# A hybrid encoder layer on one core: how 256-column products read their moving operand, and how a norm writes its parts

## The chip, the cores and the metric

The kernel runs on one core of a Trainium2 chip. The metric is the device time of one execution in microseconds (us), without anything that the host does before it: weights are arranged on the host, outside the time. Five engines work side by side, each with its own queue in program order: the TensorE (PE) for matmuls, with its weight loads (PEld); the VectorE (DVE); the ScalarE (ACT); the GpSimd (POOL); and the SyncE (SP), which here issues DMAs. Matmuls read a stationary operand (the weights that are loaded first) and a moving operand (whose columns stream through) from SBUF and write to PSUM, which ACT and DVE read.

## The reference

One encoder layer on a sequence of 512 positions and width 1024, in float32:

```
h  = RMSNorm(x);  q,k,v,g,u,sv,a_ret,a_sgu = split(h @ w_in)      # 512,512,1024,1024,1024,1024,1024,1024 columns
y_ret = (LayerNorm(retention(rotary(q), rotary(k), v)) * silu(g)) @ w_ret_o   # 4 heads, key 128, value 256, both directions
y_sgu = (gelu(u) * (w_spatial · LayerNorm(gelu(sv)) + b)) @ w_sgu_o           # chunks of 128 positions, 4 groups
x1 = x  + RMSNorm((sig(a_ret) * y_ret + sig(a_sgu) * y_sgu) @ w_out)
c  = conv3(RMSNorm(x1) @ w_up) + conv_b;  a,b = split(c)                     # 2 x 2816 columns, 3 taps along the sequence
y  = x1 + RMSNorm((gelu(a) * b) @ w_down)
```

## The kernel before, in words

**Products in three parts.** TensorE takes float32 here in a rounded form (`float32r`). To keep the accuracy, every operand is split into a high and a low part: `split` (lines 95 and 111) rounds a copy on ACT to get the high part and subtracts it on DVE to get the low one. Each product is then three matmuls into the same PSUM bank: high x high, high x low, low x high (`mm3`, lines 240 to 242, and the same written out elsewhere). A weight block streams in by DMA (`raw<-wall`, issued by SP), is split by ACT and DVE, and is used; `w_get` looks a few blocks ahead.

**512 and 256 columns.** Most products have a moving operand of 512 columns. Others have 256, for two reasons: a head's value width is 256, and large products are done by a scheme of seven products of half size in the place of eight (`Pair`, line 773, and `products`, line 1187), with sums and differences of operand blocks made by DVE and GpSimd (`x_forms`, `h2_forms`, `w_form`, `w_down`, `down_forms`). In a `Pair` a weight form is stationary and a 256-column block of x, or of the forms S1 to S4, moves. In the down projection the activations are stationary and 256 columns of w_down move; `add_whole` (line 1203) does the blocks left over.

**Reading in turn.** A moving operand of 512 columns is read as two halves in turn: column 0, column 256, column 1, column 257, and so on, so the product comes out with its columns in that mixed order. Where the order matters later, either the reader of PSUM takes every second column (`in_turn`) and writes the two halves in their places (`two`), or the weights were mixed on the host so that the product comes out in natural order (`_turns`). The 256-column products of the second norm's output (`h2h`, `h2l`) in `Pair.x` and in `early` also read in turn, as 128 columns out of each half of a 512-column tile. All other 256-column products read 256 neighbouring columns: the heads' `scores`, `states` and `values` (240 matmuls), `Pair` on x and its forms (1008) and on the forms S1 to S4 of the up projection (384), line 1187 (756) and line 1203 (192).

**Order of the work.** The q and k products come first, then per head v, scores, states and values among the other input products; then u (from 209 us), the two gated branches (to 430 us), the output product with the second norm (430 to 480 us), the up projection (to 690 us) and the down projection. In the second norm, `norms` (line 949 and on) makes mean squares on ACT, a reciprocal root on GpSimd and the scaled rows on DVE; `turn` transposes them on PE (line 1009) and writes for each k the high part on ACT (line 1011) and the low part on DVE (line 1014); `h2_rows` (line 1028) writes a float32 copy on ACT, from which `h2_forms` makes S1 to S4. While this goes on, PE does `early`, the first products of the up projection, each of which waits for its k's parts. The scheduler keeps each engine's program order as the code gives it, apart from a few places where the code pins it (`issue_after`).

Tiles are allocated with start offsets of 64 or 192 bytes in some pools (`hi192`, `lo64`, `AT_64`, `AT_192`), which set them apart from each other within 256 bytes.

Of the kernel before, what the change touches and what calls it, by code (L numbers as in the profile page):

```python
# [15 lines left out]
P = 128  # L16
# [31 lines left out]
def tile_block(ctx: ExitStack, tc, xT, x, wall, par, cs, wsp, bsp, gpost, gffn, out):  # L48
# [48 lines left out]
    def two(t):  # L97
        return t.rearrange("p (n c) -> p n c", n=2)

    def turns(t, f=slice(0, 256)):  # L100
        return t.rearrange("p (n c) -> p c n", n=2)[:, f, :]

    def in_turn(o):
        return o.rearrange("p (c n) -> p n c", n=2)
# [398 lines left out]
    def rotary(m):  # L503
# [4 lines left out]
        v.tensor_add(a, a, b)  # L508
        return a

    def parts(src, n, held=True):
        h_, l_ = (hi192(n), lo64(n)) if held else (blk(F32R, n), blk(F32R, n))
        split(h_, l_, src)
        return h_, l_

    hd = {}

    def prep(h):

        k = rotary(4 + h)  # L520
        kp = parts(k, "k")
        q = rotary(h)
        qp = parts(q, "q", False)
        xi = powers(tmp("xi"), xp, xn, h)
        v.tensor_mul(q, q, xi)
        hd[h] = [qp, kp, parts(q, "qx"), k]
# [54 lines left out]
    def scores(h):  # L581
        (qh, ql), (kh, kl) = hd[h][:2]
        dec = powers(tmp("dec"), dp, dn, h)
        sm = []
        for c in range(2):
            s = ps()
            n = slice(c * 256, (c + 1) * 256)
            for i in range(2):
                m = slice((2 * c + i) * P, (2 * c + i + 1) * P)
                mm3(s[:, i * 256 : (i + 1) * 256], kh[:, m], kl[:, m], qh[:, n], ql[:, n], True, True)  # L590
            m = tmp("sm")
            v.scalar_tensor_tensor(
                out=m, in0=s, scalar=DK ** -0.5, in1=dec, op0=ALU.mult, op1=ALU.mult
            )
            sm.append(parts(m, "sm"))
        return sm

    def states(h):
        nh, e = h // 2, slice((h % 2) * DV, (h % 2 + 1) * DV)
        kh, kl = hd[h][3]  # L600
        s = ps()
        for d in range(2):
            for i in range(2):
                t = 2 * d + i
                c = slice(t * P, (t + 1) * P)
                mm3(s[:, d * DV : (d + 1) * DV], kh[:, c], kl[:, c], vh[t, nh][:, e], vl[t, nh][:, e],
                    i == 0, i == 1)
        return parts(s, "st", False)

    def values(h, sm, st):  # L610
        nh, e = h // 2, slice((h % 2) * DV, (h % 2 + 1) * DV)
        xh_, xl_ = hd[h][2]
        for n2 in range(2):
            o = ps()
            for nn in range(2):
                n = 2 * n2 + nn
                oo = o[:, nn * DV : (nn + 1) * DV]
                for i in range(2):
                    c = slice(i * 256 + nn * P, i * 256 + (nn + 1) * P)
                    t = 2 * n2 + i  # L620
                    mm3(oo, sm[n2][0][:, c], sm[n2][1][:, c], vh[t, nh][:, e], vl[t, nh][:, e],
                        i == 0, False)
                c = slice(n * P, (n + 1) * P)
                d = slice((1 - n2) * DV, (2 - n2) * DV)
                mm3(oo, xh_[:, c], xl_[:, c], st[0][:, d], st[1][:, d], False, True)
            for nn in range(2):
                n = 2 * n2 + nn
                oo = o[:, nn * DV : (nn + 1) * DV]
                if (n, nh) not in o_sb:
                    o_sb[n, nh] = blk(n="o")  # L630
                bs = small("bs", 6, 4)
                v.bn_stats(out=bs, in_=oo)
                v.bn_aggr(out=mv[:, n, h, :], in_=bs)
                copy(o_sb[n, nh][:, e], oo)
        rsqrt(orstd[:, h, :], mv[:, :, h, 1], 1.0, NT)
        for n in range(NT):
            ot = o_sb[n, nh][:, e]
            v.tensor_scalar(
                out=ot, in0=ot, scalar1=mv[:, n, h, 0:1], scalar2=orstd[:, h, n : n + 1],
                op0=ALU.subtract, op1=ALU.mult,  # L640
            )
# [115 lines left out]
    class Pair:  # L757
# [3 lines left out]
        def __init__(self, func, alloc, a=None, scale=None):  # L761
            self.func, self.t, self.scale = func, [alloc(), alloc()], scale
            self.h, self.l, self.forms = a or (xh, xl, forms)
            self.b = [ps() for _ in range(3)]

        def product(self, b, act, first, w=None):
            wh, wl = w or w_get()
            o = self.b[b][:, T0]
            for k in range(4):
                c = slice(k * P, (k + 1) * P)  # L770
                h_, l_ = act(k)
                for n, (w_, a_) in enumerate(((wh, h_), (wh, l_), (wl, h_))):
                    self.last = nc.tensor.matmul(  # L773
                        o, w_[:, c], a_, start=first and k == n == 0, stop=k == 3 and n == 2,
                        skip_group_check=True,
                    )
            return o

        def x(self, first, t):
            if self.h is xh:  # L780
                return lambda k: (self.h[first + k][:, t], self.l[first + k][:, t])
            f = slice(t.start // 2, t.stop // 2)
            return lambda k: (turns(self.h[first + k], f), turns(self.l[first + k], f))

        def s(self, n):
            return lambda k: self.forms[n][k]

        def part1(self, apart=False):

            c0, c1 = self.t  # L790

            def second():
                o = self.product(1, self.x(4, T0), True)
                v.tensor_add(c0[:, T0], o, c0[:, T0])

            o = self.product(0, self.x(0, T0), True)
            copy(c0[:, T0], o)
            if not apart:
                second()
            self.product(2, self.s("S1"), True)  # L800
            o = self.product(0, self.s("S2"), False)
            copy(c1[:, T0], o)
            if apart:
                second()
            if self.scale is not None:
                v.tensor_mul(c0[:, T0], c0[:, T0], self.scale[:, T0])

        def part2(self):
            c0, c1 = self.t
            o = self.product(0, self.s("S3"), False)  # L810
            copy(c1[:, T1], o)
            v.tensor_sub(c1[:, T1], self.b[2][:, T0], c1[:, T1])
            self.w = w_get(), w_get()

        def part3(self):
            c0, c1 = self.t
            o = self.product(0, self.x(4, T1), False, self.w[0])
            if self.scale is None:
                copy(c0[:, T1], o)
            else:  # L820
                v.tensor_mul(c0[:, T1], o, self.scale[:, T1])
                nc.scalar.activation(out=c0, in_=c0, func=self.func)
            o = self.product(2, self.s("S4"), False, self.w[1])
            v.tensor_sub(c1[:, T0], o, c1[:, T0])
            if self.scale is not None:
                v.tensor_mul(c1, c1, self.scale)
                nc.scalar.activation(out=c1, in_=c1, func=self.func)
# [168 lines left out]

    h2 = []

    def both(t):
        return t.rearrange("p (c n) -> p c n", n=2)  # L1000

    def turn(t, zs):
        c = slice(t * 64, (t + 1) * 64)
        pf = []
        for n in range(2):
# [3 lines left out]
                nc.tensor.transpose(pf[-1], zs[n][:, f * P : (f + 1) * P], ident)  # L1009
            for k in range(4 * n, 4 * n + 4):  # L1010
                last = nc.scalar.activation(  # L1011
                    out=turns(h2h[k], c), in_=both(pf[k]), func=AF.Copy, scale=col(FFNG + k)
                )
                v.scalar_tensor_tensor(  # L1014
                    out=turns(h2l[k], c), in0=both(pf[k]), scalar=col(FFNG + k), in1=as32(turns(h2h[k], c)),
                    op0=ALU.mult, op1=ALU.subtract,
                )
        if t != 2:
# [3 lines left out]
    def h2_rows(t, pf):  # L1022

        for k in range(KD):
            if t == 0 and k % 2 == 0:
                h2.append(halves("h2"))
            at = (k % 2) * 256 + (t % 2) * P
            nc.scalar.activation(
                out=h2[k // 2][t // 2][:, at : at + P], in_=pf[k], func=AF.Copy, scale=col(FFNG + k)
            )  # L1030

    early_w, early_o = [], []
# [140 lines left out]
    def products(m, j, steps={}, look=LOOK, ahead=None):  # L1173

        for n, (unit, at, act) in enumerate(UNITS):
# [7 lines left out]
            for t in range(2):  # L1183
                c = slice(t * P, (t + 1) * P)
                o = m[n][:, t * 256 : (t + 1) * 256]
                for i, (a_, w_) in enumerate(((ah, wh), (ah, wl), (al, wh))):
                    nc.tensor.matmul(  # L1187
                        o, a_[:, c], w_[:, f], start=j == t == i == 0,
                        stop=j == DP - 1 and i == 2 and n not in (M2, M3, M4), skip_group_check=True,
                    )  # L1190
            steps.get(n, lambda: None)()
# [1 line left out]
    def add_whole(m, t, gs, ws, last=False):  # L1193

        c = slice(t * P, (t + 1) * P)
        for n, b in enumerate(((M2, M3), (M4, M8))[t // 2]):
            o = m[b][:, (t % 2) * 256 : (t % 2 + 1) * 256]
            for g, (wh, wl) in zip(gs, ws):
                for k in range(2):
                    f = slice(k * S + n * 256, k * S + (n + 1) * 256)  # L1200
                    ah, al = whole[2 * g + k]
                    for i, (a_, w_) in enumerate(((ah, wh), (ah, wl), (al, wh))):
                        nc.tensor.matmul(  # L1203
                            o, a_[:, c], w_[:, f], start=b == M8 and t == 2 and g == k == i == 0,
                            stop=last and g == gs[-1] and k == 1 and i == 2, skip_group_check=True,
                        )

# [162 lines left out]
    return a.reshape(a.shape[0] // P, P, a.shape[1])  # L1370


def _turns(a):

    return a.reshape(*a.shape[:-1], 256, 2).swapaxes(-1, -2)


def _pairs(a):
# [108 lines left out]
```

## Time and profile before

| | before |
|---|---|
| time, median of 3 runs | 806.9 us (806.28, 806.9, 809.85) |
| the profiled execution | 809.66 us, span 807.9 us |
| PE busy | 791.6 us, 98% of the span |
| PE weight loads | 735.3 us, 91% |
| DVE busy | 664.9 us, 82% |
| ACT busy | 443.3 us, 55% |
| GpSimd busy | 84.8 us, 11% |
| DMA | 93.24 MB, mean 115 GB/s |

A row of a group reads: line, engine, operation, what is written and from what, the shape, how many, busy time in us, mean duration in ns, idle time before it and what ended it. A row of the timeline reads: start in us, duration in us, engine, line, operation, tiles, shape, how many in a row, and in brackets the idle time before it and who ended that. A row of the chain that ended last gives start, length, engine, tile, line and count. Matmuls overlap, so the listed duration of one is longer than the distance to the next.

### The profile page before, as it was taken

To read this page: it belongs to the slowest core of one execution; us is meant where nothing else is said; L and a number is where in the kernel's file an instruction comes from. 1 tells how busy PE (TensorE), PEld (TensorE's weight loads), DVE (VectorE), ACT (ScalarE), POOL (GpSimd) and SP (SyncE) were. 2 spreads that over 40 slices of the span, in tenths; PEclk is the share of its full clock that TensorE was granted. 3 is DMA by queue.
4 is the path that set the end of the run, shared out by engine and by line. 5 is a ranking of instruction groups with operands and counts; after the bars stand their busy time and mean duration, and the time that the engine had idled before them with its cause. 6 is when DMAs were issued, how large, how long until landed. Compare 5 with 4: busy or idle time off the path is not lost. (4 is left out here: it accounts for less than half of the span.)

```text
span 807.9 us, 13298 instructions
## 1 busy us (share of the span) xinstructions
PE 791.6 (98%) x5163; PEld 735.3 (91%) x5163; DVE 664.9 (82%) x1115; ACT 443.3 (55%) x777; POOL 84.8 (11%) x93
## 2 busy tenths in 40 slices
PE   9989999999999999999999999999999999999996
PEld 7878998998999999999998898899998898999996
DVE  6579897877898787777765669999999989987887
ACT  6455446546676444444444687556656666544442
POOL 0010000010001111132211210110110100000001
PEclk9999999999999999999999999999999999999999
DMA  7743222222233333223359111323333341233244
GB/s 271 249 149 105 72 85 59 79 87 77 105 105 105 105 105 104 80 105 105 124 164 335 54 47 61 105 105 105 105 105 105 105 157 53 79 131 105 97 165 157
DMA packets 29903, 93.24 MB, mean 115 GB/s; under 512 B 3536, under 2 KB 4688, under 8 KB 29840
## 3 DMA queue, kind: packets, MB, share of 16 engines
q1 hardware_dynamic: 27616, 86.76, 31.4%
q0 software_dynamic: 1360, 4.46, 1.6%
q10 hardware_dynamic: 864, 1.18, 0.4%
q8 instruction: 40, 0.66, 0.3%
q14 instruction: 23, 0.19, 0.1%
HBM read 88.19 MB, written 4.19 MB: 114 GB/s over the span
## 5 line engine op out<-in xcount | busy, mean ns | idle before, releaser
L95 ACT ACTIVATE wf<-raw 128x512 fp32r<-128x512 f32 x140 | 85.4, 625 | 97.9 <-PE ps L241 30.6
L111 DVE TENSOR_TENSOR wl<-raw,wh 128x1024 fp32r<-128x1024 f32 (+1 forms) x92 | 109.6, 1200 | 34.0 <-PE ps L773 19.1
L111 DVE TENSOR_TENSOR wf<-raw,wf 128x512 fp32r<-128x512 f32 x140 | 108.7, 788 | 19.9 <-ACT wf L95 18.9
L773 PE MATMUL ps<-sh,wf 128*128 128x256 f32 x640 | 120.9, 278 | 2.0 <-ACT c L95 2.0
L95 ACT ACTIVATE wh<-raw 128x1024 fp32r<-128x1024 f32 (+2 forms) x96 | 93.0, 980 | 31.0 <-DMA raw<-wall 16.0
L773 PEld LDWEIGHTS ps<-sh,wf 128*128 128x128 f32 x640 | 101.7, 188 | 3.1 <-ACT c L95 2.4
L241 PE MATMUL ps<-h2l,wh 128*128 128x512 f32 (+1 forms) x256 | 90.4, 355 | 1.8 <-DVE h2l L1014 1.8
L240 PE MATMUL ps<-h2h,wh 128*128 128x512 f32 (+1 forms) x256 | 90.3, 355 | 0.1
L242 PE MATMUL ps<-h2h,wl 128*128 128x512 f32 (+1 forms) x256 | 90.1, 353 | 0.0
L773 PE MATMUL ps<-sl,wf 128*128 128x256 f32 x320 | 89.0, 278 | 0.0
L554 PE MATMUL ps<-wh,xh 128*128 128x512 f32 x192 | 73.5, 383 | 0.0
L556 PE MATMUL ps<-wh,xl 128*128 128x512 f32 x192 | 73.5, 383 | 0.0
L555 PE MATMUL ps<-wl,xh 128*128 128x512 f32 x192 | 73.4, 382 | 0.0
L773 PEld LDWEIGHTS ps<-sl,wf 128*128 128x128 f32 x320 | 60.1, 188 | 0.4
L1187 PE MATMUL ps<-dl,fh 128*128 128x256 f32 x216 | 59.8, 277 | 0.0
L1187 PE MATMUL ps<-dh,fh 128*128 128x256 f32 x216 | 59.7, 277 | 0.0
L1187 PE MATMUL ps<-dh,fl 128*128 128x256 f32 x216 | 59.7, 277 | 0.0
L241 PEld LDWEIGHTS ps<-h2l,wh 128*128 128x128 f32 x256 | 48.5, 189 | 6.8 <-DVE h2l L1014 2.2
L773 PE MATMUL ps<-xh,wf 128*128 128x256 f32 x288 | 54.5, 279 | 0.0
L95 ACT ACTIVATE dh<-raw 128x768 fp32r<-128x768 f32 (+1 forms) x36 | 33.6, 948 | 37.1 <-DVE raw L213 17.7
L242 PEld LDWEIGHTS ps<-h2h,wl 128*128 128x128 f32 x256 | 48.5, 190 | 5.2
L240 PEld LDWEIGHTS ps<-h2h,wh 128*128 128x128 f32 x256 | 48.3, 189 | 5.2 <-ACT h2h L1011 0.4
(314 smaller groups left out, 2037.1 us busy)
## 6 DMA issues: line engine op xcount, KB each, us to landing
raw<-wall SPq DMA_DIRECT2D x144, 512.0 KB, 3.6
x<-x SPq DMA_DIRECT2D x24, 256.0 KB, 6.0
x<-x POOLq DMA_DIRECT2D x8, 256.0 KB, 2.4
xT<-xT SPq DMA_DIRECT2D x7, 256.0 KB, 5.8
xT<-xT POOLq DMA_DIRECT2D x4, 256.0 KB, 3.4
out<-zg SPq DMA_DIRECT2D x4, 256.0 KB, 2.0
raw<-wall SPq DMA_DIRECT2D x3, 256.0 KB, 4.2
out<-zs ACTq DMA_DIRECT2D x3, 256.0 KB, 2.3
```

The lines of the kernel that those rows point to most:

```text
L95: return nc.scalar.activation(out=o, in_=i, func=AF.Copy)
L111: nc.vector.tensor_sub(lo, src, as32(hi))
L240: nc.tensor.matmul(o, ah, bh, start=start, stop=False, skip_group_check=skip)
L241: nc.tensor.matmul(o, ah, bl, start=False, stop=False, skip_group_check=skip)
L242: nc.tensor.matmul(o, al, bh, start=False, stop=stop, skip_group_check=skip)
L554: nc.tensor.matmul(acc[t], xh[k][:, c], turns(wh[:, f]), start=k == 0, stop=False)
L555: nc.tensor.matmul(acc[t], xh[k][:, c], turns(wl[:, f]), start=False, stop=False)
L556: part_end[0] = nc.tensor.matmul(acc[t], xl[k][:, c], turns(wh[:, f]), start=False, stop=k == KD - 1)
L773: self.last = nc.tensor.matmul(o, w_[:, c], a_, start=first and k == n == 0, stop=k == 3 and n == 2, skip_group_check=True,)
L1187: nc.tensor.matmul(o, a_[:, c], w_[:, f], start=j == t == i == 0, stop=j == DP - 1 and i == 2 and n not in (M2, M3, M4), skip_group_check= ...
```

## The change

Products of 256 columns now read the moving operand as two halves in turn too: in a block of 256, column 0, column 128, column 1, column 129, and so on. Where the result has to be in natural order, what reads it from PSUM takes every second column: the evictions of `Pair` on x (`self.two`), the heads' outputs (line 634 of the kernel before, `copy(o_sb...)`), and the split of the states (`parts_in_turn`). q is split with its two halves of 256 mixed each, so that the scores come out in natural order. w_down's columns are mixed on the host, in blocks of 256. For the second norm, the parts (`h2h`, `h2l`) are written as two runs of 64 columns per transposed block, with every second column read from PSUM, where before the two halves were written alternately and PSUM was read in order; the result in SBUF is the same. The float32 copy `h2` is now mixed likewise and also written in runs of 64.

```diff
-    def turns(t, f=slice(0, 256)):
-        return t.rearrange("p (n c) -> p c n", n=2)[:, f, :]
+    def turns(t, f=None):
+        v_ = t.rearrange("p (n c) -> p c n", n=2)
+        return v_ if f is None else v_[:, f, :]
...
+    def four(t):
+        return t.rearrange("p (i n c) -> p i n c", i=2, n=2)
+
+    def four_in_turn(o):
+        return o.rearrange("p (i c n) -> p i n c", i=2, n=2)
...
+    def parts_in_turn(src, n):
+        h_, l_ = blk(F32R, n), blk(F32R, n)
+        split(four(h_), four(l_), four_in_turn(src))
+        return h_, l_
...
-        qp = parts(q, "q", False)
+        qp = parts_in_turn(q, "q")
...
-                mm3(s[:, i * 256 : (i + 1) * 256], kh[:, m], kl[:, m], qh[:, n], ql[:, n], True, True)
+                mm3(s[:, i * 256 : (i + 1) * 256], kh[:, m], kl[:, m], turns(qh[:, n]), turns(ql[:, n]), True, True)
...
-                mm3(s[:, d * DV : (d + 1) * DV], kh[:, c], kl[:, c], vh[t, nh][:, e], vl[t, nh][:, e],
+                mm3(s[:, d * DV : (d + 1) * DV], kh[:, c], kl[:, c], turns(vh[t, nh][:, e]), turns(vl[t, nh][:, e]),
                     i == 0, i == 1)
-        return parts(s, "st", False)
+        return parts_in_turn(s, "st")
...
-                mm3(oo, xh_[:, c], xl_[:, c], st[0][:, d], st[1][:, d], False, True)
+                mm3(oo, xh_[:, c], xl_[:, c], turns(st[0][:, d]), turns(st[1][:, d]), False, True)
...
-                copy(o_sb[n, nh][:, e], oo)
+                copy(two(o_sb[n, nh][:, e]), in_turn(oo))
...
+            self.two = in_turn if a is None else two
...
-            return o
+            return self.two(o)
...
-                return lambda k: (self.h[first + k][:, t], self.l[first + k][:, t])
+                return lambda k: (turns(self.h[first + k][:, t]), turns(self.l[first + k][:, t]))
...
-            return lambda k: self.forms[n][k]
+            return lambda k: [turns(i) for i in self.forms[n][k]]
...
-            copy(c0[:, T0], o)
+            copy(two(c0[:, T0]), o)
...
                 last = nc.scalar.activation(
-                    out=turns(h2h[k], c), in_=both(pf[k]), func=AF.Copy, scale=col(FFNG + k)
+                    out=two(h2h[k])[:, :, c], in_=in_turn(pf[k]), func=AF.Copy, scale=col(FFNG + k)
                 )
                 v.scalar_tensor_tensor(
-                    out=turns(h2l[k], c), in0=both(pf[k]), scalar=col(FFNG + k), in1=as32(turns(h2h[k], c)),
+                    out=two(h2l[k])[:, :, c], in0=in_turn(pf[k]), scalar=col(FFNG + k), in1=as32(two(h2h[k])[:, :, c]),
...
-            at = (k % 2) * 256 + (t % 2) * P
+            half, at = (T0, T1)[k % 2], (t % 2) * 64
             nc.scalar.activation(
-                out=h2[k // 2][t // 2][:, at : at + P], in_=pf[k], func=AF.Copy, scale=col(FFNG + k)
+                out=two(h2[k // 2][t // 2][:, half])[:, :, at : at + 64], in_=in_turn(pf[k]), func=AF.Copy, scale=col(FFNG + k)
             )
...
-                        o, a_[:, c], w_[:, f], start=j == t == i == 0,
+                        o, a_[:, c], turns(w_[:, f]), start=j == t == i == 0,
...
-                            o, a_[:, c], w_[:, f], start=b == M8 and t == 2 and g == k == i == 0,
+                            o, a_[:, c], turns(w_[:, f]), start=b == M8 and t == 2 and g == k == i == 0,
...
-        _down(i["w_down"]),
+        _down(_turns(i["w_down"], P).reshape(DFF, D)),
```

The other evictions of `Pair` (`v.tensor_add`, `v.tensor_sub`, `v.tensor_mul`, the remaining copies) change as the copy shown does: `two` around what lies in SBUF.

More of the change, by code (lines that the diff above doesn't have):

```diff
@@ L620, in values @@
                     t = 2 * n2 + i
-                    mm3(oo, sm[n2][0][:, c], sm[n2][1][:, c], vh[t, nh][:, e], vl[t, nh][:, e],
+                    mm3(oo, sm[n2][0][:, c], sm[n2][1][:, c], turns(vh[t, nh][:, e]), turns(vl[t, nh][:, e]),
                         i == 0, False)
@@ L793, in second @@
                 o = self.product(1, self.x(4, T0), True)
-                v.tensor_add(c0[:, T0], o, c0[:, T0])
+                v.tensor_add(two(c0[:, T0]), o, two(c0[:, T0]))
             o = self.product(0, self.x(0, T0), True)
-            copy(c0[:, T0], o)
+            copy(two(c0[:, T0]), o)
             if not apart:
@@ L801, in part1 @@
             o = self.product(0, self.s("S2"), False)
-            copy(c1[:, T0], o)
+            copy(two(c1[:, T0]), o)
             if apart:
@@ L810, in part2 @@
             o = self.product(0, self.s("S3"), False)
-            copy(c1[:, T1], o)
-            v.tensor_sub(c1[:, T1], self.b[2][:, T0], c1[:, T1])
+            copy(two(c1[:, T1]), o)
+            v.tensor_sub(two(c1[:, T1]), self.two(self.b[2][:, T0]), two(c1[:, T1]))
             self.w = w_get(), w_get()
@@ L818, in part3 @@
             if self.scale is None:
-                copy(c0[:, T1], o)
+                copy(two(c0[:, T1]), o)
             else:
-                v.tensor_mul(c0[:, T1], o, self.scale[:, T1])
+                v.tensor_mul(two(c0[:, T1]), o, two(self.scale[:, T1]))
                 nc.scalar.activation(out=c0, in_=c0, func=self.func)
             o = self.product(2, self.s("S4"), False, self.w[1])
-            v.tensor_sub(c1[:, T0], o, c1[:, T0])
+            v.tensor_sub(two(c1[:, T0]), o, two(c1[:, T0]))
             if self.scale is not None:
@@ L997, in tile_block @@
     h2 = []
-    def both(t):
-        return t.rearrange("p (c n) -> p c n", n=2)
     def turn(t, zs):
@@ L1370, in _rows, with _turns @@
     return a.reshape(a.shape[0] // P, P, a.shape[1])
-def _turns(a):
-    return a.reshape(*a.shape[:-1], 256, 2).swapaxes(-1, -2)
+def _turns(a, n=256):
+    return a.reshape(*a.shape[:-1], -1, n, 2).swapaxes(-1, -2)
 def _pairs(a):
```

## The prediction

> **What bounds the kernel now.** I read the shares of busy time first, then busy time by stage, then who waited for whom on the TensorE (PE).
>
> ```profile
> span 807.9 us, 13298 instructions
> PE 791.6 (98%) x5163; PEld 735.3 (91%) x5163; DVE 664.9 (82%) x1115; ACT 443.3 (55%) x777; POOL 84.8 (11%) x93
> ```
> ```profile
> core 0: us, PE busy (x) PEld busy (x) DVE busy (x) ACT busy (x) POOL busy (x), PEclk, DMA share, GB/s
> 75.00:195.00 120.00, 120.00 (x677) 108.69 (x677) 101.48 (x182) 62.76 (x95) 9.67 (x16) 1.00 0.25 82
> ...
> 260.00:430.00 170.00, 170.00 (x1108) 158.77 (x1107) 125.29 (x189) 78.60 (x132) 32.64 (x23) 1.00 0.35 115
> 510.00:690.00 180.00, 177.29 (x1129) 163.74 (x1128) 173.31 (x271) 111.49 (x191) 20.67 (x14) 1.00 0.32 106
> 690.00:745.00 55.00, 55.00 (x473) 54.67 (x472) 45.53 (x74) 27.59 (x37) 1.13 (x2) 1.00 0.33 109
> ```
> ```profile
> engine line waited for: us in total, times, longest us
> PE ps L449 <- ACT qkraw L95: 2.9, 1, 2.9
> PE ps L773 <- ACT c L95: 2.7, 3, 1.0
> PE ps L241 <- DVE h2l L1014: 1.8, 2, 1.0
> ```
>
> PE is busy 791.6 of 807.9 us, at full granted clock in every stage shown, and from 75 to 195 and from 260 to 430 us it never rests. It waits only a few times, 2.9 us at most. So what counts is how far apart matmuls start. A matmul's listed duration (278 ns for 256 columns) overlaps the next one and is no price; the price is the distance between starts. One engine comes near PE: VectorE (DVE), 173.3 of 180 us busy in the up projection (510 to 690).
>
> **The price of a 256-column product, both ways of reading, in this trace.** Line 773 already has both. With h2h as the moving operand it reads the two halves in turn (`turns`); with sh it reads 256 neighbouring columns. These rows are the first of a run of 24 in turn, the first of the 24 contiguous ones that follow, and the instruction behind those:
>
> ```profile
> 529.57 0.27 PE L773 MATMUL ps<-h2h,wf 128*128 128x256 f32 x1
> 532.25 0.28 PE L773 MATMUL ps<-sh,wf 128*128 128x256 f32 x1
> 534.98 0.38 PE L240 MATMUL ps<-h2h,wh 128*128 128x512 f32 x1
> ```
>
> (532.25-529.57)/24 = 111.7 ns in turn; (534.98-532.25)/24 = 113.8 ns contiguous, with weights of the same kind. Other contiguous runs on that line (312, 48 and 24 products), and a head's 36:
>
> ```profile
> 209.59 0.28 PE L773 MATMUL ps<-xh,wf 128*128 128x256 f32 x1
> 244.96 0.38 PE L696 MATMUL ps<-ident,o 128*128 128x128 f32 x2
> ...
> 271.19 0.36 PE L773 MATMUL ps<-xh,wf 128*128 128x256 f32 x1
> 276.98 0.38 PE L240 MATMUL ps<-gh,wh 128*128 128x512 f32 x1
> ...
> 412.25 0.28 PE L773 MATMUL ps<-xh,wf 128*128 128x256 f32 x1
> 415.10 0.38 PE L240 MATMUL ps<-yh,wh 128*128 128x512 f32 x1
> ```
> ```profile
> 87.29 0.28 PE L240 MATMUL ps<-vh,sm 128*128 128x256 f32 x1
> 91.57 0.38 PE L554 MATMUL ps<-wh,xh 128*128 128x512 f32 x1
> ```
>
> 113.4, 120.6 and 118.8 ns; the head 118.9. The 26 such runs from 209.59 to 415.10 us (1008 products) average 115.4, each steady in itself. The down projection stands in the chain that ended last, as start, length and count:
>
> ```profile
> 692.76 19.32 PE ps L1187 x168
> 712.08 5.44 PE ps L1203 x48
> ...
> 732.48 55.99 PE ps L1187 x492
> ```
>
> 80.75 us for these 708 products: 114.1 ns.
>
> **The change, part by part.** No instruction is added, removed or moved: each engine's queue and both DMA-issuing queues hold the same instructions in the same order. Only access patterns differ, and the order of w_down's columns, arranged on the host outside the measured time.
>
> 1. *The matmuls.* 2580 products go from contiguous to in turn. At 111.7 ns each:
>  - heads (scores, states, values): 240 x (118.9-111.7) = 1.7 us.
>  - u, sigmoid and gate pairs (L773, 195 to 430 us): 1008 x (115.4-111.7) = 3.7 us. PE does not wait there.
>  - S1 to S4 of the up projection: 384 x 3.7 = 1.4 us, the 3.7 taken from the row above (the run shown here would give 2.1 each, 0.8 us).
>  - down (L1187, L1203): 948 x (114.1-111.7) = 2.3 us.
>
>  Together 9.1 us, all on PE. What the trace lacks is the distance: wherever it reads in turn, a half is 256 columns (1024 bytes) from the other, and the new patterns have them 128 columns (512 bytes) apart. Bounds from the nearest rows: 111.7 (no matter) and 120.6 (as the costliest contiguous run shown, which would add 2580 x 5.4 = 14 us to the mean of 115.2 that the four groups have now). I take 111.7: the nearest row is the same instruction with the same weights and output, and both distances are multiples of 256 bytes, so that the offsets of 64 and 192 bytes by which the kernel sets its tiles apart stay what they are.
>
> 2. *The evictions.* Pairs of x, the heads' outputs and the states leave PSUM with every second column read. Rows with that pattern (qkraw, r) and without (gh, e):
>
> ```profile
> L95 ACT ACTIVATE gh<-ps 128x512 fp32r<-128x512 f32 x8 | 4.3, 592 | 0.0
> L95 ACT ACTIVATE qkraw<-ps 128x512 f32<-128x512 f32 x4 | 2.0, 593 | 0.0
> L900 DVE TENSOR_TENSOR r<-ps,sig 128x512 f32<-128x512 f32 x8 | 5.4, 688 | 1.5 <-ACT sig L822 0.8 <-PE ps L242 0.5
> L1345 DVE TENSOR_TENSOR e<-ps,e 128x512 f32<-128x512 f32 x1 | 0.7, 684 | 0.0
> ```
>
>  1 ns on ACT, 4 on DVE: nothing. For q the split reads every second column of SBUF, which no row here shows alone. Lower bound nothing; upper bound twice a 128x512 split, some 1.3 us a head. It is covered: `prep(h+1)` runs a head ahead and DVE has 18.5 us free in 75 to 195. Without that cover 5 us would show as a wait of the scores.
>
> 3. *The norm's parts* (`turn`). Before, they are written alternately into two halves; then, in two runs of 64.
>
> ```profile
> L1011 ACT ACTIVATE h2h<-ps,part 128x128 fp32r<-128x128 f32 x32 | 14.6, 492 | 6.6 <-DVE h2l L1014 6.2 <-PE ps L1009 0.2
> L1014 DVE SCALAR_TENSOR_TENSOR h2l<-ps,part,h2h 128x128 fp32r<-128x128 f32 x32 | 13.5, 442 | 5.8 <-ACT h2h L1011 5.4
> L1028 ACT ACTIVATE h<-ps,part 128x128 f32<-128x128 f32 x32 | 8.8, 392 | 0.3 <-DVE h2l L1014 0.3
> L848 DVE SCALAR_TENSOR_TENSOR add<-rws,part,bst x8: 337/344/1370, 257.1 to 337.9; 128x128 f32<-128x128 f32 x8
> 475.51 3.95 ACT L1011 ACTIVATE h2h<-ps,part 128x128 fp32r<-128x128 f32 x8 [0.18 <-PE ps L1009]
> 476.02 3.92 DVE L1014 SCALAR_TENSOR_TENSOR h2l<-ps,part,h2h 128x128 fp32r<-128x128 f32 x8 [0.22 <-ACT h2h L1011]
> 463.00 0.38 PE L241 MATMUL ps<-h2l,wh 128*128 128x256 f32 x1 [0.76 <-DVE h2l L1014]
> 465.63 0.38 PE L241 MATMUL ps<-h2l,wh 128*128 128x256 f32 x1 [1.03 <-DVE h2l L1014]
> ```
>
>  Same size with contiguous output: 392 on ACT (L1028), median 344 on DVE (L848); so about 100 ns off each of the 64 writes. The last eight k go out 3.95/8 = 494 ns apart and PE (3 x 111.7 = 335 ns per k) follows that pace: 8 x 0.1 = 0.8 us off the path. The two waits of 0.76 and 1.03 us sit behind chains with several of these writes; I give 0.5. Sum 1.3 us; bounds 0 (runs of 64 cost what alternation costs) and 3.1 (both waits gone, 1.8, and the last eight at PE's pace, 3.95-8 x 0.335 = 1.3). The f32 copies for the forms (L1028) change from contiguous to runs of 64: between nothing and 100 ns on 32 writes. I take nothing, since 64 columns of a run lie side by side as L1028's 128 do; the dear end would put up to 0.8 us (eight of them) into ACT's queue ahead of the last norm's squares, on which the last transposes wait.
>
> **What of it stays.** DVE carries the chain through part of the up projection:
>
> ```profile
> 596.93 0.68 DVE gp L1084
> ...
> 635.65 0.28 ACT c L95
> ```
>
> From 596.93 to 635.65 that chain is DVE, ACT and GpSimd, and two of PE's waits for ACT's c (1.0 us each) lie in it. There a faster PE only waits longer. I keep half of that stage's 1.4. Next late after the change: DVE in the up projection. Sum: 1.7 + 3.7 + 0.7 + 2.3 + 1.3 = 9.7 us. The profiled execution took 809.66 us (span 807.9), so the same one would take 800.0; it is 2.8 above the median of the runs, so 806.9-9.7 = **797.2 us**.
>
> **Rivals.**
> - *Reading 512 bytes apart is slower than contiguous.* Place: all 2580 products. Counting the norm's 1.3 us, it ends slower than before once they average over 115.2 + 0.5 = 115.7 ns. At the 120.6 of the costliest run shown: 806.9 + 13.9-1.3 = 819.5 us. Against it: 111.7 at 1024 bytes, where each column also lies far from the one before. [...] 10%.
> - *The reading gains nothing at 512 bytes*, the products keep their times, and only the norm counts: 806.9-1.3 = 805.6. For it: nothing in the trace names the cause of the 111.7. 9%.
> - *DVE sets the pace from 500 us on*, so up and down give nothing: 806.9-1.7-3.7-1.3 = 800.2. For it: 173.3 of 180. Against: 9.5 us free in 690 to 745, and PE never waits there. 11%.
>
> **How the numbers follow.** The forecast has 70%; its own range is 794.7 to 799.2 (norm 3.1 and up whole, or neither). A measurement of this kernel can tell about 0.5%, 4 us. Faster by more: forecast and third rival, 81%; within: 9%; slower: 10%. The range runs from 794.2 (the forecast's low end and half a us of scatter) to 803.5, past the third rival and towards the second.
>
> **What would show it.** In turn everywhere: starts 111.7 apart in the heads, L773, L1187 and L1203, with no run at 118 or 120. Norm: h2h near 390, h2l near 350, the last eight h2h in about 3.1 us. Evictions: unchanged within 5 ns. The waits for ACT's c should stay or grow a little. Wrong would make it: starts above 115 ns, new PE waits behind sig, u or o evictions, or those waits growing by as much as PE gains.

## The result and the profile after

| | before | after |
|---|---|---|
| median of 6 runs | 806.72 us (806.12 to 809.85) | 798.13 us (797.19 to 800.58) |
| ratio to before | | 0.9886 (95% interval 0.9863 to 0.9909) |
| the profiled execution | 809.66 us | 797.19 us |

The change makes the kernel 8.6 us faster; the forecast was 9.7 us (797.2 us). Two rows of the page of after, the span and the shares of busy time:

```profile
span 795.4 us, 13304 instructions
PE 782.7 (98%) x5163; PEld 727.3 (91%) x5163; DVE 661.7 (83%) x1115; ACT 440.1 (55%) x777; POOL 85.2 (11%) x93
```

TensorE (PE) executes the same 5163 matmuls and is still the bound. The timeline of after shows the distances between starts. In order: a head's 36 products (84.24 to 88.26), a run of 312 products of x pairs (205.13 to 239.97) and 24 products of a form S of the up projection (521.64 to 524.32); each second row is the instruction behind the run.

```profile
84.24 0.27 PE L241 MATMUL ps<-vh,sm 128*128 128x256 f32 x1
88.26 0.38 PE L566 MATMUL ps<-wh,xh 128*128 128x512 f32 x1
...
205.13 0.27 PE L786 MATMUL ps<-xh,wf 128*128 128x256 f32 x1
239.97 1.04 PE L708 MATMUL ps<-ident,o 128*128 128x128 f32 x8
...
521.64 0.28 PE L786 MATMUL ps<-sh,wf 128*128 128x256 f32 x1
524.32 0.38 PE L241 MATMUL ps<-h2h,wh 128*128 128x512 f32 x1
```

The three are (88.26-84.24)/36 = 111.7, (239.97-205.13)/312 = 111.7 and (524.32-521.64)/24 = 111.7 ns. The down projection in the chain that ended last (start, length, count):

```profile
706.52 9.38 PE ps L1197 x84
715.90 5.36 PE ps L1213 x48
721.26 54.94 PE ps L1197 x492
776.20 2.69 PE ps L1213 x24
```

54.94/492 = 111.7 ns, 113.8 before for the same 492 (55.99 us). So every run of 256-column products now keeps the distance of the ones that were read in turn before; none at 118 or 120 is left. The groups of the norm's writes, and the last eight k of them on the timeline:

```profile
L1021 ACT ACTIVATE h2h<-ps,part 128x128 fp32r<-128x128 f32 x32 | 11.2, 368 | 6.6 <-DVE h2l L1024 5.6 <-PE ps L1019 0.6
L1024 DVE SCALAR_TENSOR_TENSOR h2l<-ps,part,h2h 128x128 fp32r<-128x128 f32 x32 | 10.8, 347 | 4.6 <-ACT h2h L1021 4.0
L1038 ACT ACTIVATE h<-ps,part 128x128 f32<-128x128 f32 x32 | 8.8, 396 | 0.2 <-DVE h2l L1024 0.2
```
```profile
465.84 3.17 ACT L1021 ACTIVATE h2h<-ps,part 128x128 fp32r<-128x128 f32 x8 [0.58 <-PE ps L1019]
```

The high parts cost 368 ns where they cost 492, the low parts 347 where they cost 442, and the f32 copy costs the same (392 and 396). The waits of PE of after:

```profile
engine line waited for: us in total, times, longest us
PE ps L786 <- ACT c L95: 3.0, 3, 1.2
PE ps L336 <- PEq L1487: 0.8, 1, 0.8
PE ps L242 <- DVE h2l L1024: 0.7, 1, 0.7
PE ps L354 <- ACT xh L275: 0.5, 1, 0.5
PE ps L1197 <- DVE dl L112: 0.3, 1, 0.3
```

Against before: the waits for the low part fell from 1.8 to 0.7 us, those for ACT's c in the up projection grew from 2.7 to 3.0, one for dl in the down projection is new, and the 2.9 us for qkraw are gone. That last one is no part of the change. It lies near 50 us, ahead of the first changed instruction (q's split, at 62.6 us in after), and differs between executions: a profile of the changed kernel with other tile offsets (experiment 5) has 1.7 us of it, and that of experiment 2, which up to there is the kernel before, has 0.3.

**Where the time went, matmul by matmul.** Both traces hold the same 5163 matmuls in the same order, so the start of the n-th in one can be subtracted from that in the other. Times of the first column are those of before.

| stretch | gain of after, us | forecast |
|---|---|---|
| start, to 55 us (nothing changed there) | 2.92 | - |
| heads, to 209 | 1.55 | 1.7 |
| pairs of u, sigmoid and gate, to 448 | 3.75 | 3.7 |
| output product, second norm and early products, to 485 | 2.31 | 1.3 |
| up projection, to 692 | 0.60 | 0.7 |
| down projection, to the end | 1.32 | 2.3 |

Without the start that is 9.53 us; with it 12.45, and the two profiled executions are 12.47 apart. The 2.92 of the start are 1.9 us that after loses in its first 8 us, 3.0 that it gains at the wait for qkraw, and 1.8 that it gains behind that wait: there the granted clock of before falls, to 0.89 from 50 to 52 us, 0.50 from 52 to 54 and 0.75 from 54 to 56. The ratio's interval is a gain of 7.3 to 11.1 us (806.72 times one minus its ends), so 9.5 and 9.7 are both inside, and the third rival's 6.7 is not. Each stretch is read from one profile of each kernel, and some of them scatter by a few tenths of a us, as the experiments show.

### The profile page after: what moved, and what is told of

Same layout as the page of the kernel before. It is cut to its first block, busy times and chain, and to the rows that moved or that the text cites. A ratio compares the mean times of both kernels' runs of the same rounds, so it can differ in the third digit from the quotient of the medians.

```text
span 795.4 us, 13304 instructions
## 1 busy us (share of the span) xinstructions
PE 782.7 (98%) x5163; PEld 727.3 (91%) x5163; DVE 661.7 (83%) x1115; ACT 440.1 (55%) x777; POOL 85.2 (11%) x93
## 5 line engine op out<-in xcount | busy, mean ns | idle before, releaser
L786 PE MATMUL ps<-sh,wf 128*128 128x256 f32 x640 | 117.5, 276 | 2.6 <-ACT c L95 2.3
L786 PE MATMUL ps<-xh,wf 128*128 128x256 f32 x288 | 52.8, 277 | 0.0
```

Source lines behind the costliest of these rows:

```text
L786: self.last = nc.tensor.matmul(o, w_[:, c], a_, start=first and k == n == 0, stop=k == 3 and n == 2, skip_group_check=True,)
```

## The experiments

Each measured time stands beside that of the kernel before, from runs on the same chip. Experiments 1, 2 and 10 have 6 to 12 runs; the others have one each and are read from their traces.

**1 and 2: which of the two parts brings what.** Experiment 1 is the changed kernel with the norm's parts written alternately again; experiment 2 is the kernel before with only the runs of 64.

```diff
# 1, on after (h2l likewise)
-                    out=two(h2h[k])[:, :, c], in_=in_turn(pf[k]), func=AF.Copy, scale=col(FFNG + k)
+                    out=turns(h2h[k], c), in_=pf[k].rearrange("p (c n) -> p c n", n=2), func=AF.Copy, scale=col(FFNG + k)
# 2, on before (h2l likewise)
-                    out=turns(h2h[k], c), in_=both(pf[k]), func=AF.Copy, scale=col(FFNG + k)
+                    out=two(h2h[k])[:, :, c], in_=in_turn(pf[k]), func=AF.Copy, scale=col(FFNG + k)
```

> The changed kernel with one part undone: the norm's parts h2h and h2l are written alternately into the two halves again, as before. The products all read in turn. If the forecast's split is right (norm 1.3 us, bounds 0 to 3.1), this runs 1 to 2.5 us behind the changed kernel and about 7 us ahead of the kernel before; h2h near 490 ns and h2l near 440, the last eight h2h in 3.95 us. If the norm's part is worth nothing, it equals the changed kernel, and the 2.3 us by which the stage from the last output products to the end of the early products shrank came from elsewhere.

> The kernel before with the norm's part alone: h2h and h2l written in runs of 64, all 256-column products that read contiguously still do. If the parts add, it gains 1 to 2.5 us on the kernel before (ratio 0.997 to 0.999) and the starts of the contiguous runs stay at 113 to 122 ns. If the whole gain came from the norm, it would come near the changed kernel, 8 to 9 us.

Measured beside 807.02 us of before: experiment 1 799.76 us (ratio 0.9897, 0.9871 to 0.9923), experiment 2 804.25 us (0.9964, 0.9949 to 0.998). The groups of experiment 1 and of experiment 2, and the wait for the low part in 1:

```profile
L1021 ACT ACTIVATE h2h<-ps,part 128x128 fp32r<-128x128 f32 x32 | 14.6, 490 | 6.6 <-DVE h2l L1024 6.2 <-PE ps L1019 0.2
```
```profile
L1011 ACT ACTIVATE h2h<-ps,part 128x128 fp32r<-128x128 f32 x32 | 11.3, 367 | 6.6 <-DVE h2l L1014 5.3 <-PE ps L1009 0.6
```
```profile
PE ps L242 <- DVE h2l L1024: 1.8, 2, 1.0
```

The durations and the wait go with the way of writing and with nothing else: 490 ns and 1.8 us where it is undone, 367 where it stands alone. The matmuls bring 7.3 us by themselves, the norm 2.8; their sum of 10.1 lies within the interval of the whole. The 2.8 (interval 1.6 to 4.1) is above the 1 to 2.5 expected of experiment 2; on top of the matmuls, from experiment 1 to after, the medians differ by 1.6, as expected. Matmul by matmul, the norm's stretch differs by 2.6 us between experiment 1 and after, and by 2.7 between before and experiment 2; in the latter 0.7 us are given back in the up projection.

**3 and 4: is it the alternation itself?** All 256-column products of the pairs (on x and on S) and of the down projection read in another order: as four quarters in turn (3), or the even columns first and then the odd ones (4). Only `turns` is exchanged at these places.

```diff
+    def other(t):
+        return t.rearrange("p (n c) -> p c n", n=4)      # 3
+        return t.rearrange("p (c n) -> p n c", n=2)      # 4
...
-            return lambda k: [turns(i) for i in self.forms[n][k]]
+            return lambda k: [other(i) for i in self.forms[n][k]]
...
-                        o, a_[:, c], turns(w_[:, f]), start=j == t == i == 0,
+                        o, a_[:, c], other(w_[:, f]), start=j == t == i == 0,
```

> The changed kernel, but the 256-column products of the pairs on x and S1 to S4 and of the down projection read four quarters in turn (64 columns, 256 bytes apart) in the place of two halves, so the order of their columns is wrong. Theory one: what helps is that the moving stream advances through each half no faster than the next weight load does; four streams advance slower still, and the starts stay at 111.6 ns or within 0.5 of it. Theory two: two halves are special (each line of neighbouring columns met every other time); then four cost more, 113 ns or above. [...]

> The changed kernel, but the same products (pairs on x and S1 to S4, down projection) read the even columns of a block first and then the odd ones, so the order of their columns is wrong. The moving stream then runs through the 1024 bytes twice, at twice the speed of contiguous reading. Theory one (a stream slower through memory is better): starts above the contiguous 113 to 122 ns. Theory two (any order in which neighbours are not read one after the other is as good): 111.6 ns.

Measured: 859.24 and 1067.32 us, beside 807.02. The chain that ended last, first of 3 and then of 4, the run of 312 x pairs and the 492 products of the down projection:

```profile
203.31 43.69 PE ps L789 x312
...
764.40 70.41 PE ps L1200 x492
```
```profile
204.92 72.13 PE ps L789 x312
...
920.42 113.11 PE ps L1200 x492
```

Quarters: 43.69/312 = 140.0 and 70.41/492 = 143.1 ns; every second column: 231 and 230 ns. So "columns far apart" is neither good nor bad as such, and more streams are not better: two streams read column by column are the cheapest of these orders (111.7 ns), four are 28 to 31 ns dearer, and steps of two columns in one stream cost twice as much.

**5 and 6: the tiles' offsets.** The offsets of 64 and 192 bytes are taken away, from after (5) and from before (6).

```diff
-    pads = {"hi192": 16, "lo64": 32}
+    pads = {}
...
-    AT_64, AT_192 = 16, 48
+    AT_64, AT_192 = 0, 0
```

> The changed kernel with the start offsets of 64 and 192 bytes taken away from the weight tiles and the hi192 and lo64 pools, so that nearly all moving and stationary operands start at the same place within 256 bytes. If reading in turn is cheap because the two operands are set apart, its starts rise above 111.6 ns, by some ns, and the 512-column ones above 216. If reading in turn makes the offsets irrelevant, 111.6 and 216 stay and the time equals the changed kernel's.

> The kernel before with the same offsets taken away. Contiguous 256-column products cost 113 to 122 ns there, each run steady in itself. If the place of the two operands within 256 bytes sets which, the cost changes for all runs together, up by several ns (2580 products: +5 ns is 13 us). If something else sets it (where tiles lie farther apart, or what other engines do), the spread 113 to 122 stays.

Measured beside 806.57 us: 797.6 (after without offsets) and 816.02 (before without offsets). The 492 products of the down projection in the chain of 5, and in that of 6:

```profile
721.58 55.02 PE ps L1197 x492
```
```profile
735.15 58.97 PE ps L1187 x492
```

Read in turn, they keep 111.8 ns. Read contiguously, 58.97/492 = 119.9 ns in the place of 113.8, and the heads, pairs and up projection move to 119 to 120 as well. Late first products aside, the contiguous runs of before lie between 113.4 and 119.0 ns and those of experiment 6 between 118.5 and 120.1; behind the start its trace is 10.5 us behind that of before. So what a contiguous product costs depends on its tiles' start offsets, and the spread in the trace of before goes when they go. In turn, the cost does not depend on them (111.7 ns with them, 111.8 without). Which offsets of the two operands make 113.8 and which 119 the record does not show, as the traces hold no addresses, and offsets may not be all of it: three runs of 12 products of a form S (at 600.3, 621.5 and 642.7 us of before) cost 113.8 ns there and 119 in experiment 2, whose offsets in the code are the same. Experiment 5 also carries the wait for qkraw named above:

```profile
PE ps L450 <- ACT qkraw L95: 1.7, 1, 1.7
```

**7: does the VectorE (DVE) hold back the up projection?** The changed kernel without one of the three taps of the convolution, 44 DVE instructions of 0.74 us.

```diff
-        v.scalar_tensor_tensor(
-            out=c[:, 0 : S - 1], in0=o[:, 1:S], scalar=col(CW + 3 * m + 2), in1=c[:, 0 : S - 1],
-            op0=ALU.mult, op1=ALU.add,
-        )
```

> The changed kernel with one of the three convolution taps left out: the second of the two DVE instructions of conv (44 of 0.74 us), so DVE has some 30 us less to do in the up projection. If DVE's backlog makes the waits for ACT's c (3.0 us in the list of waits, with the slow restarts behind them near 4) and the first waits for dl in the down projection, they go, and the kernel gains 4 to 5 us and not more, since PE sets the rest. If ACT's own queue makes them, they stay and the time is within 1 us. If DVE sets the pace more widely, the gain is much more than 5 us.

Measured: 790.03 us, beside 806.57. The busy time by stage (length, then PE, PEld, DVE, ACT and GpSimd), first of after, then of experiment 7:

```profile
510.00:690.00 180.00, 176.90 (x1149) 163.42 (x1148) 174.05 (x275) 111.01 (x188) 20.58 (x14) 1.00 0.29 100
690.00:745.00 55.00, 54.66 (x489) 54.37 (x488) 46.59 (x77) 28.05 (x47) 1.13 (x2) 1.00 0.36 120
```
```profile
510.00:690.00 180.00, 180.00 (x1196) 167.98 (x1195) 155.29 (x251) 116.44 (x195) 19.10 (x15) 1.00 0.34 109
```

With DVE at 155.3 of 180 us PE doesn't rest at all, and its waits for c and for dl are gone. Against before, matmul by matmul, the up projection gains 5.16 us (0.60 in after) and the down projection 2.09 (1.32 in after). The expectation of 4 to 5 us was a little low: beyond the start, which differs by 1.5 us, this profile is 5.75 us ahead of after. Of these, 0.42 arise at 456 us at the wait for the low part, which is 0.3 us where after has 0.7; the first convolution starts only at 473.8 us, so that much is scatter between executions and not the tap. DVE's work is what PE waits for in the up projection and at the start of the down projection.

**8 and 9: distance, number of streams, neighbours.** Other orders in the pairs on x, in the forms S and in the down projection, one each.

```diff
# 8: two streams 256 bytes apart | two streams 128 bytes apart | four streams 512 bytes apart
+        return t.rearrange("p (m n c) -> p m c n", m=2, n=2)
+        return t.rearrange("p (m n c) -> p m c n", m=4, n=2)
+        return w_[:, :512].rearrange("p (n c) -> p c n", n=4)[:, :64, :]
# 9: two neighbours of each half in turn | four neighbours of each half in turn | eight streams
+        return t.rearrange("p (n c b) -> p c n b", n=2, b=2)
+        return t.rearrange("p (n c b) -> p c n b", n=2, b=4)
+        return w_[:, f].rearrange("p (n c) -> p c n", n=8)
```

> The changed kernel with three other orders of reading, one per group of 256-column products, so columns come out in a wrong order (and in the down projection partly other columns are read). Pairs on x: two streams 64 columns (256 bytes) apart, one block of 128 columns after the other. S1 to S4: two streams 32 columns (128 bytes) apart, four blocks. Down: four streams 128 columns (512 bytes) apart. The quarters cost 140 and 143 ns with four streams 256 bytes apart. If the number of streams makes that, x and S stay at 111.6 and down is near 143. If the distance of 256 bytes makes it, x is near 140, S 140 or above, and down 111.6. The heads, unchanged, stay at 111.6.

> The changed kernel with three other orders, columns come out in a wrong order. Pairs on x: two neighbouring columns of one half, then two of the other. S1 to S4: four neighbours (16 bytes) of one half, then four of the other. Down: eight streams 32 columns (128 bytes) apart. Reading even columns and then odd ones cost 229 ns, about twice the contiguous 114: each piece of memory is visited twice. [...] Down: above 143 by both the number of streams and the distance.

Measured: 825.07 and 933.95 us, beside 807.02. From the timeline of 8, 12 products of x and 12 of S with the row behind each; and the down projection in its chain:

```profile
203.83 0.27 PE L795 MATMUL ps<-xh,wf 128*128 128x256 f32 x1
205.17 0.28 PE L795 MATMUL ps<-sh,wf 128*128 128x256 f32 x1
...
507.11 0.27 PE L795 MATMUL ps<-sh,wf 128*128 128x256 f32 x1
508.45 0.38 PE L250 MATMUL ps<-h2h,wh 128*128 128x512 f32 x1
```
```profile
730.24 70.41 PE ps L1206 x492
```

And the same of 9:

```profile
205.26 0.33 PE L795 MATMUL ps<-xh,wf 128*128 128x256 f32 x1
207.29 0.29 PE L795 MATMUL ps<-sh,wf 128*128 128x256 f32 x1
...
562.73 0.29 PE L795 MATMUL ps<-sh,wf 128*128 128x256 f32 x1
564.24 0.38 PE L250 MATMUL ps<-h2h,wh 128*128 128x512 f32 x1
```
```profile
792.96 108.28 PE ps L1206 x492
```

| order | ns per product |
|---|---|
| two streams in turn, 128, 256, 512 or 1024 bytes apart | 111.7 |
| contiguous | 113 to 120, by the tiles' offsets at least |
| four neighbours of each half in turn | 126 |
| four streams, 256 or 512 bytes apart | 140 to 143 |
| two neighbours of each half in turn | 165 to 169 |
| eight streams | 220 |
| every second column | 229 to 231 |

The 169 is a run of 12 products; the median of all with two neighbours of each half is 165. The distance between the streams doesn't matter from 128 to 1024 bytes; their number does, and so does taking exactly one column from each in turn. No run shows what inside the chip makes this list, so the cause stays open.

**10: can the up projection be arranged around the wait?** The first four of a pair's seven products are issued between the convolutions of the two tiles of the pair ahead, where they were behind both.

```diff
+    def up_pair():
+        p = Pair(None, lambda: tmp("c"), (h2h, h2l, h2forms))
+        p.part1()
+        return p
...
+            p, ahead_ = ahead_, None
+            if p is None:
+                p = up_pair()
...
+            if i + 2 in couples:
+                ahead_ = up_pair()
```

> The changed kernel, output unchanged, with one move in the up projection: the first part of the next pair (its weight forms, its first four products and the copy c that PE waits for) is issued between the two tiles' convolutions of the pair before, not behind both. If ACT's order behind DVE's backlog makes PE's waits for c (3.0 us and some restarts), they shrink and the kernel gains 2 to 4 us on the changed one (795 us, ratio to the kernel before 0.984 to 0.987). If DVE's total work sets the stage, the waits only move to other places and the time stays within 1 us.

Measured: 799.98 us beside 807.02, ratio 0.9914 (0.9893 to 0.9935), so no gain over after's 0.9886; the intervals overlap, and its trace is 2.4 us behind that of after, more than the 1 us expected. The waits of PE:

```profile
PE ps L786 <- ACT c L95: 2.5, 2, 1.6
PE ps L786 <- DVE c L825: 1.8, 2, 1.4
PE ps L1207 <- DVE dl L112: 1.4, 2, 1.0
```

They sum to 5.7 us where after has 3.3 for c and dl. The order of the work moves PE's waits to other places, but DVE has as much to do as before (from 500 to 690 us it is busy for 181.8 us, 184.0 in after) and PE waits for it there.

**11: products of 512 columns.** On after: the group of v, sv and g reads its 512 columns contiguously, and the output product reads them as four quarters in turn.

```diff
-                    nc.tensor.matmul(acc[t], xh[k][:, c], turns(wh[:, f]), start=k == 0, stop=False)
+                    nc.tensor.matmul(acc[t], xh[k][:, c], wh[:, f], start=k == 0, stop=False)
...
-            nc.tensor.matmul(o, ah, turns(bh), start=k == 0, stop=False)
+            nc.tensor.matmul(o, ah, quarters(bh), start=k == 0, stop=False)
```

> The changed kernel with two groups of 512-column products read in another order, so their columns come out in a wrong order: the 576 of v, sv and g contiguously, the 192 of the output product as four quarters in turn (128 columns, 512 bytes apart). In turn they cost 216 ns each. Contiguous 256-column products cost 2 to 10 ns more than in turn. If that is a cost per product, the 512-column ones go to 218 to 226 (576 x 2 to 10 = 1 to 6 us); if it grows with the columns, to 220 to 236 (2 to 12 us). Quarters cost 28 to 31 ns more at 256 columns; with the columns that is some 60 at 512, about 275 ns, and 192 x 60 = 11 us.

Measured: 815.76 us beside 807.29. The timeline, two contiguous products 23 apart, then two of the output product 17 apart:

```profile
202.65 0.39 PE L569 MATMUL ps<-wh,xh 128*128 128x512 f32 x1
207.87 0.39 PE L571 MATMUL ps<-wh,xl 128*128 128x512 f32 x1
...
447.78 0.45 PE L956 MATMUL ps<-wh,ml 128*128 128x512 f32 x1
452.59 0.45 PE L955 MATMUL ps<-wl,mh 128*128 128x512 f32 x1
```

(207.87-202.65)/23 = 227.0 ns contiguous and (452.59-447.78)/17 = 282.9 ns as quarters, where all of them took 216 in turn. Contiguous reading costs 11 ns more, so of the two bounds expected the one that grows with the columns holds (220 to 236 ns); quarters cost 67 more. So at 512 columns, too, two streams are the cheapest of the three.

## Why the prediction was right, and where it was off

- *The distance of 512 bytes.* The prediction took 111.7 ns because the nearest row had it at 1024 bytes; after has 111.7 everywhere, and experiment 8 shows that even 128 bytes would have done. The first rival (dearer than contiguous at 512 bytes) and the second (no gain there) are refuted. The 120.6 ns that the prediction takes as the costliest run has a late first product of 201 ns in it; the run's other products are 119.0 apart. The forecast does not rest on it.
- *Heads and pairs.* 1.55 and 3.75 us against 1.7 and 3.7. Starts multiplied by counts gave the gain, since PE never waits in these stages.
- *The up projection.* "I keep half of that stage's 1.4" gave 0.7; 0.60 came. The reason holds: PE's waits for c grew to 3.0 us, and experiment 7 shows that they go when DVE has less to do. Outside the waits the S products fell from 115.6 to 111.6 ns, 1.5 us in all, and some 0.9 of it went into longer waits and the slow products behind them (in after the first one behind such a wait takes 213 to 215 ns). The half itself was a guess, and that it came so near is luck: the same stretch gains 0.06 us in experiment 1 and 0.03 in experiment 5, which read S in turn as well.
- *The down projection: mis-sized.* The term was 948 x (114.1-111.7) = 2.3 us, and 1.32 came. Two things are in the difference. The 114.1 was the mean of the 708 products in the rows shown; the other 240 are 113.3 ns apart and all of them 113.9, which makes the term 2.1. And the step said that PE never waits there. With PE earlier, it does, for dl, which DVE writes; the timeline of after:

```profile
697.71 0.28 PE L1197 MATMUL ps<-dh,fh 128*128 128x256 f32 x1
698.33 0.38 PE L1197 MATMUL ps<-dl,fh 128*128 128x256 f32 x1 [0.34 <-DVE dl L112]
698.54 0.28 PE L1197 MATMUL ps<-dh,fl 128*128 128x256 f32 x1
```

 From 697.71 to 698.54 two products take 0.83 us where 0.22 would do, and a smaller stall at 692.9 costs 0.16; together 0.77. With DVE relieved (experiment 7) the down projection gains 2.09. So the third rival, DVE's pace from 500 us on, was partly true: it took over half of the up projection's 1.4 and about a third of the down projection's 2.1, not all.
- *The norm: too low, inside its bounds.* 1.3 us were forecast between 0 and 3.1; the stretch gained 2.31, and the pairs of traces with and without the runs of 64 say 2.6 and 2.7. The 100 ns per write were about right (124 and 95). The last eight writes go out in 3.17 us, 0.78 sooner, as forecast (0.8). The waits for the low part gave 1.1 (1.8 to 0.7), not 0.5: each stands behind a chain of several such writes, and with every write 0.1 shorter one of the two waits went altogether. Some 0.4 us of the 2.31 are not assigned to a row. In experiment 1, with the matmuls alone, this stretch is 0.3 behind before.
- *The evictions.* From PSUM, every second column costs nothing, as forecast (o: 379 ns in both). The states' split shows it with the pattern that q's split has: 596 ns on ACT before and 593 after, 691 and 690 on DVE. q's split reads SBUF; it was bounded, not seen, and it does cost something. Its rows in before and in after:

```profile
L95 ACT ACTIVATE q<-rot 128x512 fp32r<-128x512 f32 x4 | 2.5, 633 | 5.6 <-DVE rot L508 5.6
L111 DVE TENSOR_TENSOR q<-rot,q 128x512 fp32r<-128x512 f32 x4 | 2.7, 685 | 0.0
```
```profile
L95 ACT ACTIVATE q<-rot 128x512 fp32r<-128x512 f32 x4 | 3.3, 834 | 5.9 <-DVE rot L509 5.9
L112 DVE TENSOR_TENSOR q<-rot,q 128x512 fp32r<-128x512 f32 x4 | 3.3, 823 | 0.1
```

 That is 0.34 us a head, inside the bound of 1.3, and PE has no wait for q in the heads.

The sum came out at 9.5 against 9.7 since the norm's extra 1.0 us and the down projection's missing 1.0 cancel. That the sum came so near is luck; that reading in turn makes most of the gain is not, as experiment 1 shows.

## What to carry to other kernels

Price matmuls by the distance between starts, and look for the same instruction under two access patterns in the trace you have: that comparison carried nearly the whole forecast. Of the orders tried for a rounded float32 moving operand, two halves read column by column in turn is the cheapest (111.7 ns at 256 columns), and unlike the contiguous order it cost the same with the kernel's tile offsets and without them (111.7 and 111.8); the other orders were tried with one placement only. Measure before going to another number of streams (four cost 140 to 143 ns here, eight 220). Where another engine was at 97% of a stage (DVE in the up projection here), the faster bound engine lost most of its gain in that stage to waits (0.9 of 1.5 us); the one reordering tried moved the waits, while taking work off the other engine removed them.

## What the runs showed that was not expected

- What a contiguous 256-column product costs depends on its tiles' start offsets: without the kernel's offsets 119 to 120 ns, with them 113.8 in most of the down projection, and 816.02 us in the place of 806.57 for the kernel before (one run each). The kernel after needs no offsets (797.6 us without, one run).
- The floor of 111.7 ns (216 ns at 512 columns). Late first products and waits aside, the mean of any run of 256-column products of rounded float32 in after is 111.4 to 111.7 ns, and none of the orders tried goes below that. What sets it no run shows.
- Writing 128 columns of rounded float32 alternately into two halves costs ACT 124 ns and DVE 95 ns more than writing them in runs of 64 (492 against 368 and 442 against 347), while reading every second column from PSUM costs nothing that shows (593 ns against 596 for the states' split on ACT). Reading every second column from SBUF does: 201 ns more on ACT and 138 on DVE for 512 columns.
- Behind its wait of 2.9 us the trace of before lost another 1.8 us, while the granted clock was down to 0.50 (52 to 54 us); behind the wait of 1.7 us in experiment 5 the clock stayed at 1.00 (45 to 75 us). With the matmuls behind it, the wait in the trace of before is to be priced at 4.7 us in the place of 2.9.
